# Merge-gate projections of a two-layer encoder in pairs, by seven half-size products

## The chip, the cores and the metric

The kernel runs on one core of a Trainium2 chip. The core has engines that work side by side, each through its own list of instructions in a fixed order: TensorE (PE) multiplies matrices, VectorE (DVE) and ScalarE (ACT) work element by element, GpSimd (POOL) does so too and issues some DMAs, SyncE (SP) issues most DMAs. Operands lie in SBUF, products are summed up in PSUM, the weights and the larger intermediates lie in DRAM. An instruction waits, with all behind it on its engine, until semaphores say that its inputs are there and its buffer is free. The metric is the time of one execution in microseconds (us).

## What is computed

The reference has two layers. In each, all branches read the same normalised input h through one projection, and three sigmoid gates join the branches:

```
h = rmsnorm(x, g_norm)
z = einsum('bsd,dn->bsn', h, w_in)
dq, dk, dv, dg, lq, lk, lv, lg, mq, mg, mgate = split(z, splits)
o_a = diff_attention(...) ; y_a = (rmsnorm(o_a) * (1 - lam_init) * silu(dg)) @ w_br_diff
o_b = dilated groups, combined ; y_b = (o_b * silu(lg)) @ w_br_dil
o_m = memory_attention(...) ; y_m = (o_m * silu(mg)) @ w_br_mem
gates = sigmoid(mgate).reshape(B, S, 3, 1024)
merged = gates[:, :, 0] * y_a + gates[:, :, 1] * y_b + gates[:, :, 2] * y_m
x = x + merged @ w_out
```

There are 512 tokens, a width of 1024 and fp32 throughout; the result is rmsnorm(x, g_final) behind the second layer.

## The kernel before

Each fp32 matrix is kept as two parts, hi and lo, and each product is formed by three matmuls (hi x hi, lo x hi, hi x lo: `mm3`, lines 166 to 169). `split` (lines 94 to 96) makes hi on ACT and lo on DVE. hT, the transposed h, stays in SBUF as hT_hi and hT_lo: 8 blocks of 128 rows with 512 tokens. A projection of 128 columns of w_in (`proj_fm`) is 8 x 3 = 24 matmuls of a 128x128 stationary tile with 512 columns into one PSUM tile. The PSUM tiles with the tag "mm" are 4, taken in turn.

Weights come in the order of `weight_order`. `prefetch` keeps LEAD = 2 weights ahead of the one in use: a DMA into w_raw (3 buffers), w_hi by ACT (4 buffers), w_lo by DVE (3 buffers). A split so waits until PE has done with the weight three or four before it.

A layer has these stages: hT from x; the memory's keys and values; differential, dilated and memory attention woven together, whose results (o_sb, f_osb) go to DRAM in u_d and v_d; and `merge` (lines 580 to 622). `merge` begins with 16 gate projections in U_ORDER, called the U projections below (the U stage). For each, a stored branch result is loaded (u_raw, for 8 of them also a norm u_v with a square root on ACT), the gate is sigmoid on ACT (line 183) and a product on DVE that reads the PSUM tile again (line 184), then u_raw times gate (line 592), u_hi and u_lo. Sigmoid and square root are in different tables of ACT, with a table load at each change. Then come 8 blocks d: three merge-gate projections with a sigmoid each (lines 600 to 604), ya (24 matmuls with w_br_diff), ym and yb (24 matmuls), three products and two sums on DVE, and a split of the sum into mg_hi and mg_lo. `out_proj` multiplies these with w_out.

The Python code yields the instructions; the framework's scheduler, with a model of the times that is used while the kernel is built, decides where each of them stands on its engine, and so also how far the first instructions of the U stage move up among the last ones of attention. In the order, names carry a number for each tile. On the way out of the dilated attention, d_o is its last PSUM tile, and o_sb_5320 (before) or o_sb_5357 (after) the copy of it.

## Time and profile before

| | |
|---|---|
| time, median of 3 runs | 1769.75 us (1768.26 to 1772.07) |
| the profiled execution | 1770.44 us, its span 1768.4 us |
| PE busy | 1743.8 us (99%) |
| DVE, ACT, POOL busy | 1005.5 (57%), 834.5 (47%), 22.1 us (1%) |

Busy time is the time in which an engine executes. PE's matmuls are pipelined, so the durations of neighbours overlap, and what one costs is the distance from its start to the next. An idle engine costs nothing as long as the chain of work that ends last doesn't run over it.

### The profile page before, as it was taken

The page shows a single profiled execution, that of the slowest core. Times are in us where ns is not written, and L with a number is a line of the kernel's source. Part 1 is how long each engine was busy: PE and PEld are TensorE (multiplying, and loading weights), DVE is VectorE, ACT ScalarE, POOL GpSimd, SP SyncE. Part 2 cuts the span into 40 slices and gives each one's busy share as a digit, 9 for nine tenths or more (in the row PEclk, how much of TensorE's full clock was granted, in tenths as well). Part 3 has the DMA queues.
Part 4 walks back from the last instruction along what each step waited for, and adds up shares of the span by engine and source line. Part 5 has one row for each costly group of instructions (what it writes and reads, how often), then busy time and mean ns, then how long its engine had stood idle before and what let it go on. Part 6 is the DMA issues. An engine that isn't in the chain of part 4 may idle for free.

```text
span 1768.4 us, 23429 instructions
## 1 busy us (share of the span) xinstructions
PE 1743.8 (99%) x9012; PEld 1496.0 (85%) x9012; DVE 1005.5 (57%) x1727; ACT 834.5 (47%) x1436; POOL 22.1 (1%) x45
## 2 busy tenths in 40 slices
PE   7999999999999999999999999999999999999998
PEld 6798889888888888888888898888988888888886
DVE  6566576666765663333465656658566747333333
ACT  6455555545555642222255555455454548322223
POOL 2200000000000000000000000000000000000000
PEclk9999999999999999999999999999999999999999
DMA  9643243332432643333572333324332336333342
GB/s 263 141 130 86 72 123 89 103 94 76 117 97 80 202 138 95 97 93 116 160 199 59 112 85 103 94 76 116 95 98 86 101 109 202 107 96 95 96 154 72
DMA packets 308847, 200.26 MB, mean 113 GB/s; under 512 B 14116, under 2 KB 283428, under 8 KB 308736
## 3 DMA queue, kind: packets, MB, share of 16 engines
...
## 4 chain that ended last, share of the span: by engine, by line
PE 97%; DMA 1%; ACT 1%; DVE 0%; issue 0%; SPq 0%; DVEq 0%; ACTq 0%
PE mm L167 27%; PE mm L169 27%; PE mm L168 27%; PE wT_ps L384 2%; PE f_s L407 2%; PE f_s L408 2%; DMA w_raw<-in_w_mem_kv 1%; PE f_o L168 1%; PE f_o L169 1%; PE f_o L167 1%; PE d_o L533 1%; PE d_s L509 1%; PE w_ps L522 0%; PE d_o L168 0%; PE d_o L169 0%; PE d_o L167 0%
## 5 line engine op out<-in xcount | busy, mean ns | idle before, releaser
L96 DVE TENSOR_TENSOR w_lo<-w_raw,w_hi 128x1024 fp32r<-128x1024 f32 (+2 forms) x296 | 335.8, 1135 | 436.1 <-PE mm L169 389.7
L95 ACT ACTIVATE w_hi<-w_raw 128x1024 fp32r<-128x1024 f32 (+2 forms) x296 | 293.3, 991 | 601.5 <-PE mm L168 296.0
L167 PE MATMUL mm<-hT_hi,w_hi 128*128 128x512 f32 x1344 | 529.9, 395 | 1.9 <-ACT hT_hi L95 1.9
L169 PE MATMUL mm<-hT_hi,w_lo 128*128 128x512 f32 x1344 | 527.3, 392 | 0.0
L168 PE MATMUL mm<-hT_lo,w_hi 128*128 128x512 f32 x1344 | 526.7, 392 | 0.0
L167 PEld LDWEIGHTS mm<-hT_hi,w_hi 128*128 128x128 f32 x1344 | 252.8, 188 | 53.2 <-ACT hT_hi L95 2.1
L169 PEld LDWEIGHTS mm<-hT_hi,w_lo 128*128 128x128 f32 x1344 | 252.9, 188 | 53.0 <-DVE w_lo L96 0.4
L168 PEld LDWEIGHTS mm<-hT_lo,w_hi 128*128 128x128 f32 x1344 | 253.0, 188 | 50.7
L169 PE MATMUL mm<-w_hi,hT_lo 128*128 128x384 f32 (+1 forms) x512 | 160.8, 315 | 0.0
L167 PE MATMUL mm<-w_hi,hT_hi 128*128 128x384 f32 (+1 forms) x512 | 160.0, 313 | 0.0
L168 PE MATMUL mm<-w_lo,hT_hi 128*128 128x384 f32 (+1 forms) x512 | 158.5, 310 | 0.0
L413 ACT ACTIVATE f_e<-f_e,f_st 128x512 f32<-128x512 f32 x128 | 91.9, 721 | 49.7 <-DVE f_st L410 49.7
L167 PE MATMUL mm<-u_hi,w_hi 128*128 128x512 f32 x256 | 101.2, 395 | 0.0
L169 PE MATMUL mm<-u_hi,w_lo 128*128 128x512 f32 x256 | 101.2, 395 | 0.0
L168 PE MATMUL mm<-u_lo,w_hi 128*128 128x512 f32 x256 | 101.1, 395 | 0.0
L167 PEld LDWEIGHTS mm<-w_hi,hT_hi 128*128 128x128 f32 x512 | 96.9, 189 | 1.0
L168 PEld LDWEIGHTS mm<-w_lo,hT_hi 128*128 128x128 f32 x512 | 96.8, 189 | 1.1
L169 PEld LDWEIGHTS mm<-w_hi,hT_lo 128*128 128x128 f32 x512 | 96.7, 189 | 0.0
L410 DVE CUSTOM_DVE_ANT_0 f_e<-f_s,f_bias 128x512 f32<-128x512 f32 x128 | 84.4, 681 | 6.8 <-PE f_s L408 6.7
L96 DVE TENSOR_TENSOR f_wTlo<-wT_ps,f_wThi 128x512 fp32r<-128x512 f32 x64 | 43.7, 683 | 31.4 <-ACT f_wThi L95 30.2
L615 DVE TENSOR_TENSOR mgate<-mm,mgate 128x512 f32<-128x512 f32 x48 | 33.0, 688 | 48.4 <-PE mm L169 48.4
L447 DVE RECIPROCAL f_sq<-f_sq 128x512 f32<-128x512 f32 x16 | 53.6, 3349 | 9.5 <-ACT f_sq L446 9.5
(203 smaller groups left out, 2403.9 us busy)
## 6 DMA issues: line engine op xcount, KB each, us to landing
w_raw<-in_w_in SPq DMA_DIRECT2D x168, 512.0 KB, 3.8
...
```

The lines of the kernel that those rows point to most:

```text
L95: nc.scalar.activation(hi, src, AF.Copy)
L96: nc.vector.tensor_tensor(out=lo, in0=src, in1=f32(hi), op=ALU.subtract)
L167: nc.tensor.matmul(o, lhsT=lh, rhs=rh, start=start, stop=False)
L168: nc.tensor.matmul(o, lhsT=lh, rhs=rl, start=False, stop=False)
L169: nc.tensor.matmul(o, lhsT=ll, rhs=rh, start=False, stop=stop)
L384: nc.tensor.transpose(t[:, i], s, ident)
L407: nc.tensor.matmul(sp, lhsT=qh[:, cs], rhs=K[s, m], start=True, stop=False)
L408: nc.tensor.matmul(sp, lhsT=ql[:, cs], rhs=K[s, m], start=False, stop=True)
L410: nc.vector.tensor_tensor_reduce(out=em.rearrange("p (c b) -> p c b", c=4), in0=sp, in1=bt[:, 3 - c:7 - c], op0=ALU.add, op1=ALU.min, scal ...
L413: nc.scalar.activation(em, em, AF.Exp, scale=-1.0, bias=stt[:, m:m + 1], accum_out=stt[:, 2 + m:3 + m])
L447: nc.vector.reciprocal(sq, sq)
L615: nc.vector.tensor_tensor(out=g, in0=y, in1=g, op=ALU.mult)
```

## The change

A pair of merge-gate projections is a product of a matrix of 256 weight columns (2 x 128) and 1024 rows with hT. Cut in halves each way (columns A and B; rows 0 to 511 and 512 to 1023; tokens 0 to 255 and 256 to 511), it is a 2x2 by 2x2 product of blocks, and the change forms it with seven products of blocks in place of eight. Each product has 4 blocks of 128 rows, so 4 x 3 = 12 matmuls with 256 columns.

- `load_pair` loads the four weight blocks of a pair and forms four sums of them on POOL; `prefetch` splits the seven blocks in four parts (three tiles of 1024 elements a partition, one of 512).
- `right_sums` forms the four sums T0 to T3 of blocks of hT on DVE (20 operations) and stores them in t_d in DRAM; it is woven into the attention, but the scheduler puts the operations of it straight behind hT. `right_operands` loads them in 8 tiles t_in in `merge` and splits them (T0hi to T3hi and T0lo to T3lo, each in two halves).
- `pair` adds the products into two tiles on DVE; the sigmoid is taken from there. `merge_steps` orders three pairs and two y steps (ya, ym and yb as before) for two blocks d, and the weights follow that order.
- u_raw, u_v, m and xr share 8 buffers (u_raw and u_v had 3 each). The sums m stay as fp32 until the last pair, and are then split into hT_hi and hT_lo, which `out_proj` reads.

```
+def merge_steps(d0):
+    d1 = d0 + 1
+    return (("pair", (d0, 0), (d0, 1)), ("pair", (d0, 2), (d1, 2)), ("y", d0), ("pair", (d1, 0), (d1, 1)), ("y", d1))
+LAST_PAIR = ((7, 0), (7, 1))
...
+    t_d = dr.tile([4, 2, 128, 2, 256], F32, name="t_d")
...
+    def load_pair(key):
+        l, cols = key[1], key[2:]
+        pool = pair_pool[0]
+        t1, t2, t3 = [pool.tile([128, 8, 128], F32, tag="raw", name="s_raw", bufs=4) if i < 2 else
+                      wp.tile([128, 8, 128], F32, tag="raw", name="s_raw3", bufs=3) for i in range(3)]
+        t4 = pool.tile([128, 4, 128], F32, tag="raw4", name="s_raw4", bufs=2)
+        lo, up = slice(0, 4), slice(4, 8)
+        for t, part, f, k in ((t2, lo, 1, 0), (t3, up, 1, 1), (t1, lo, 0, 0), (t3, lo, 0, 1)):
+            src = w_in[l, k * 512:(k + 1) * 512, cols[f]:cols[f] + 128]
+            dma(t[:, part], src.rearrange("(k p) n -> p k n", p=128))
+        a11, a21, a12, a22 = t1[:, lo], t2[:, lo], t3[:, lo], t3[:, up]
+        tt = nc.gpsimd.tensor_tensor
+        tt(out=t2[:, up], in0=a21, in1=a22, op=ALU.add)
+        tt(out=t1[:, up], in0=t2[:, up], in1=a11, op=ALU.subtract)
+        tt(out=a21, in0=a11, in1=a21, op=ALU.subtract)
+        tt(out=t4, in0=a12, in1=t1[:, up], op=ALU.subtract)
+        for i, t in enumerate((t1, t2, t3, t4)):
+            loaded.append((key + (i,), t))
...
+        if pair_pool and len(loaded) < 3 and order and order[0][0] == "pair":
+            load()
...
+    def pair(l, colA, colB, B, gA, gB):
+        (b11, b21, b22), T = B
+        units = {}
+        def prod(u, part, rhs):
+            if u not in units:
+                units[u] = weight("pair", l, colA, colB, u)
+            (hi, lo), (rh, rl) = units[u], rhs
+            o = mm([128, S], name="s_mm")[:, 0:256]
+            for k in range(4):
+                kk = 4 * part + k
+                mm3(o, hi[:, kk], lo[:, kk], rh[:, k], rl[:, k], k == 0, k == 3)
+            return o
+        add = lambda out, x, y: nc.vector.tensor_tensor(out=out, in0=x, in1=y, op=ALU.add)
+        c11, c12, c21, c22 = gA[:, H0], gA[:, H1], gB[:, H0], gB[:, H1]
+        nc.scalar.activation(c11, prod(0, 0, b11), AF.Copy)
+        add(c12, prod(0, 1, T[1]), c11)
+        add(c21, prod(1, 0, T[2]), c12)
+        o = prod(1, 1, T[0])
+        add(c22, o, c21)
+        add(c12, o, c12)
+        add(c11, prod(2, 0, b21), c11)
+        add(c21, prod(2, 1, T[3]), c21)
+        add(c12, prod(3, 0, b22), c12)
+    H0, H1 = slice(0, 256), slice(256, 512)
+    def right_sums(pool):
+        def acc(out, x, y, op):
+            nc.vector.tensor_tensor(out=out, in0=x, in1=y, op=op)
+        for k2 in range(2):
+            def quarter(kh, ts):
+                ks = slice(4 * kh + 2 * k2, 4 * kh + 2 * k2 + 2)
+                return f32(hT_hi[:, ks, ts]), f32(hT_lo[:, ks, ts])
+            b11, b12, b21, b22 = quarter(0, H0), quarter(0, H1), quarter(1, H0), quarter(1, H1)
+            t1, t2, t3, t4 = [pool.tile([128, 2, 256], F32, tag="ts", name="t_sum", bufs=4) for _ in range(4)]
+            for t, x, y in ((t1, b12, b11), (t3, b22, b12)):
+                acc(t, x[0], y[0], ALU.subtract)
+                yield
+                acc(t, t, x[1], ALU.add)
+                yield
+                acc(t, t, y[1], ALU.subtract)
+                yield
+            for t, x, y in ((t2, b22, t1), (t4, b21, t2)):
+                acc(t, x[0], y, ALU.subtract)
+                yield
+                acc(t, t, x[1], ALU.add)
+                yield
+            for i, t in enumerate((t1, t2, t3, t4)):
+                dma(t_d[i, k2], t)
+            yield
+    def right_operands(pool):
+        T = [[pool.tile([128, 4, 256], F32R, name=f"T{i}{p}") for p in ("hi", "lo")] for i in range(4)]
+        quarter = lambda ks, ts: (hT_hi[:, ks, ts], hT_lo[:, ks, ts])
+        k1, k2 = slice(0, 4), slice(4, 8)
+        yield (quarter(k1, H0), quarter(k2, H0), quarter(k2, H1)), T
+        loads = []
+        for k2 in range(2):
+            for i in range(4):
+                t = pool.tile([128, 2, 256], F32, tag="uT", name="t_in", bufs=32)
+                dma(t, t_d[i, k2])
+                loads.append((T[i], slice(2 * k2, 2 * k2 + 2), t))
+        yield
+        for (hi, lo), ks, t in loads:
+            split(hi[:, ks], lo[:, ks], t)
+            yield
...
     def merge(l, yu, ym, lam_init):
         U = {}
-        for i in U_ORDER:
-            raw = yu.tile([128, S], F32, tag="ul", name="u_raw", bufs=3)
+        pair_pool[:] = [yu]
+        rop = right_operands(yu)
+        B = next(rop)
+        m_tile = lambda name: ym.tile([128, S], F32, tag="m", name=name, bufs=8)
+        for n, i in enumerate(U_ORDER):
+            next(rop, None)
+            raw = m_tile("u_raw")
             dma(raw, u_d[i])
             if i < 8:
-                v = yu.tile([128, S], F32, tag="uv", name="u_v", bufs=3)
+                v = m_tile("u_v")
                 dma(v, v_d[i])
...
+        M, G = [], {}
+        for d0 in range(0, 8, 2):
+            for step in merge_steps(d0):
+                if step[0] == "pair":
+                    gA, gB = [sg_tile(name="mgate") for _ in range(2)]
+                    pair(l, *[MGATE + b * 1024 + d * 128 for d, b in step[1:]], B, gA, gB)
+                    for g in (gA, gB):
+                        nc.scalar.activation(g, g, AF.Sigmoid)
+                    G[step[1]], G[step[2]] = gA, gB
+                    if step[1:] == LAST_PAIR:
+                        for e, m in enumerate(M):
+                            split(hT_hi[:, e], hT_lo[:, e], m)
+                    continue
+                d = step[1]
+                gs = [G.pop((d, b)) for b in range(3)]
...
+                m = m_tile("m")
+                nc.vector.tensor_tensor(out=m, in0=gs[0], in1=gs[2], op=ALU.add)
+                M.append(m)
+                if d == 7:
+                    split(hT_hi[:, d], hT_lo[:, d], m)
+        pair_pool[:] = []
...
-                            mm3(os[c], M[kk][0][:, cs], M[kk][1][:, cs], whi[:, k], wlo[:, k], kk == 0, kk == 7)
+                            mm3(os[c], hT_hi[:, kk, cs], hT_lo[:, kk, cs], whi[:, k], wlo[:, k], kk == 0, kk == 7)
...
-                xr = ym.tile([128, 512], F32, tag="xr", name="xr", bufs=2)
+                xr = ym.tile([128, 512], F32, tag="m", name="xr", bufs=8)
...
-                fp, _ = weave((diff_proj(l, j + 1, P), 8), (dil_att(l, j, P, dp), 4))
+                gens = [(diff_proj(l, j + 1, P), 8), (dil_att(l, j, P, dp), 4)]
+                if j == 1:
+                    gens.append((right_sums(al), 22))
+                fp = weave(*gens)[0]
...
-    nc = bacc.Bacc("TRN2", target_bir_lowering=False, num_devices=1)
+    nc = bacc.Bacc("TRN2", target_bir_lowering=False, num_devices=1, dynamic_dma_scratch_size=2048)
```

In this order all rows are of layer 0; layer 1 has them alike. The first place is ACT where the attention ends and the U stage begins. Before, from o_sb, the copy of the last dilated attention result, on:

```order
L189 ACTIVATE o_sb_5320<-d_o_5181 128x512
L95 ACTIVATE u_hi_5394<-u_raw_5357 128x512
L183 ACTIVATE gate_5648<-mm_5623 128x512
L95 ACTIVATE u_hi_5435<-u_raw_5398 128x512
L183 ACTIVATE gate_5693<-mm_5668 128x512
L95 ACTIVATE w_hi_5795<-w_raw_5793 128x1024
```

After, from the instruction behind o_sb on:

```order
L105 ACTIVATE w_hi_5872<-w_raw_5870 128x1024
L105 ACTIVATE T0hi_5394<-t_in_5402 128x512
L105 ACTIVATE T1hi_5396<-t_in_5404 128x512
L105 ACTIVATE T2hi_5398<-t_in_5406 128x512
L105 ACTIVATE T3hi_5400<-t_in_5408 128x512
L105 ACTIVATE T0hi_5394<-t_in_5410 128x512
L105 ACTIVATE T1hi_5396<-t_in_5412 128x512
L105 ACTIVATE w_hi_5913<-w_raw_5911 128x1024
L105 ACTIVATE T2hi_5398<-t_in_5414 128x512
L105 ACTIVATE T3hi_5400<-t_in_5416 128x512
L105 ACTIVATE u_hi_5455<-u_raw_5418 128x512
L303 ACTIVATE gate_5721<-mm_5696 128x512
```

The first u_hi and the sigmoid of the 7th U projection (gate_5648 before, gate_5721 after) moved behind two weight splits and eight T splits.

The second place is DVE at the same point. Before, from the weight split of the 11th U projection on:

```order
L96 TENSOR_TENSOR w_lo_5710<-w_raw_5707,w_hi_5709 128x1024
L592 TENSOR_TENSOR u_raw_5357<-u_raw_5357,gate_5390 128x512
L592 TENSOR_TENSOR u_raw_5398<-u_raw_5398,gate_5431 128x512
L96 TENSOR_TENSOR u_lo_5395<-u_raw_5357,u_hi_5394 128x512
L184 TENSOR_TENSOR gate_5648<-mm_5623,gate_5648 128x512
L592 TENSOR_TENSOR u_raw_5439<-u_raw_5439,gate_5472 128x512
```

After, from the last but two of the first six T splits on, with the weight split of the 13th U projection, w_lo_5873:

```order
L106 TENSOR_TENSOR T3lo_5401<-t_in_5408,T3hi_5400 128x512
L106 TENSOR_TENSOR T0lo_5395<-t_in_5410,T0hi_5394 128x512
L106 TENSOR_TENSOR T1lo_5397<-t_in_5412,T1hi_5396 128x512
L106 TENSOR_TENSOR w_lo_5873<-w_raw_5870,w_hi_5872 128x1024
L106 TENSOR_TENSOR T2lo_5399<-t_in_5414,T2hi_5398 128x512
L717 TENSOR_TENSOR u_raw_5418<-u_raw_5418,gate_5451 128x512
L106 TENSOR_TENSOR T3lo_5401<-t_in_5416,T3hi_5400 128x512
L717 TENSOR_TENSOR u_raw_5461<-u_raw_5461,gate_5494 128x512
L717 TENSOR_TENSOR u_raw_5504<-u_raw_5504,gate_5537 128x512
L717 TENSOR_TENSOR u_raw_5547<-u_raw_5547,gate_5580 128x512
L106 TENSOR_TENSOR u_lo_5456<-u_raw_5418,u_hi_5455 128x512
L304 TENSOR_TENSOR gate_5721<-mm_5696,gate_5721 128x512
```

The gate product of the 7th U projection, behind which PE's 11th may write the PSUM tile, stood four places behind the weight split of the 11th and now stands eight places behind that of the 13th.

## Rows read from the trace of the kernel before

**Rows 1.** The page: busy time of engines, and the chain of waits.
```profile
PE 1743.8 (99%) x9012; PEld 1496.0 (85%) x9012; DVE 1005.5 (57%) x1727; ACT 834.5 (47%) x1436; POOL 22.1 (1%) x45
...
PE 97%; DMA 1%; ACT 1%; DVE 0%; issue 0%; SPq 0%; DVEq 0%; ACTq 0%
```

**Rows 2.** PE timeline, U stage: start us, duration us, engine, line, operation, out<-in, count.
```profile
584.51 0.40 PE L169 MATMUL mm<-hT_hi,w_lo 128*128 128x512 f32 x1
...
589.99 0.39 PE L169 MATMUL mm<-hT_hi,w_lo 128*128 128x512 f32 x1
```

**Rows 3.** PE timeline, attention of layer 0: matmuls of 256 columns.
```profile
303.66 0.28 PE L168 MATMUL f_o<-f_wTlo,f_vhi 128*128 128x256 f32 x1
303.78 0.28 PE L169 MATMUL f_o<-f_wThi,f_vlo 128*128 128x256 f32 x1
...
304.85 0.28 PE L169 MATMUL f_o<-f_wThi,f_vlo 128*128 128x256 f32 x1
```

**Rows 4.** DVE by line and form: count, busy us, mean ns, idle before and releaser.
```profile
L96 DVE TENSOR_TENSOR w_lo<-w_raw,w_hi 128x1024 fp32r<-128x1024 f32 x232 | 283.0, 1221 | 324.6 <-PE mm L169 289.3 <-PE mm L168 22.0 <-issue 9.2
...
L96 DVE TENSOR_TENSOR u_lo<-u_raw,u_hi 128x512 fp32r<-128x512 f32 x32 | 22.0, 687 | 9.3 <-ACT u_hi L95 9.0
...
L96 DVE TENSOR_TENSOR f_vlo<-mm,f_vhi 128x256 fp32r<-128x256 f32 x32 | 13.3, 420 | 3.2 <-ACT f_vhi L95 2.8
```

**Rows 5.** ACT by line and form, same columns.
```profile
L95 ACT ACTIVATE w_hi<-w_raw 128x1024 fp32r<-128x1024 f32 x232 | 245.9, 1060 | 447.0 <-issue 175.4 <-PE mm L168 163.4 <-PE mm L169 78.6
...
L603 ACT ACTIVATE mgate<-mm 128x512 f32<-128x512 f32 x48 | 27.8, 578 | 0.0
...
L588 ACT ACT_TABLE_LOAD x10 | 12.8, 1283 | 0.2
...
L95 ACT ACTIVATE f_vhi<-mm 128x256 fp32r<-128x256 f32 x32 | 11.9, 384 | 3.4 <-PE mm L169 2.7
```

**Rows 6.** ACT timeline, U stage of layer 0; idle before and releaser in brackets.
```profile
584.25 0.60 ACT L189 ACTIVATE o_sb<-d_o 128x512 f32<-128x512 f32 x1 [0.26 <-PE d_o L533]
585.02 0.63 ACT L95 ACTIVATE u_hi<-u_raw 128x512 fp32r<-128x512 f32 x1 [0.18 <-DVE u_raw L592]
585.56 0.58 ACT L183 ACTIVATE gate<-mm 128x512 f32<-128x512 f32 x1
...
588.88 1.06 ACT L95 ACTIVATE w_hi<-w_raw 128x1024 fp32r<-128x1024 f32 x1 [1.73 <-issue]
...
610.72 0.63 ACT L588 ACTIVATE u_v<-u_v 128x512 f32<-128x512 f32 x1 [3.10 <-DMA u_v<-v_d]
```

**Rows 7.** DVE timeline, U stage of layer 0.
```profile
583.16 1.23 DVE L96 TENSOR_TENSOR w_lo<-w_raw,w_hi 128x1024 fp32r<-128x1024 f32 x1 [6.43 <-PE mm L169]
584.30 1.29 DVE L592 TENSOR_TENSOR u_raw<-u_raw,gate 128x512 f32<-128x512 f32 x2
...
586.30 0.68 DVE L184 TENSOR_TENSOR gate<-mm,gate 128x512 f32<-128x512 f32 x1
...
631.13 0.69 DVE L589 SCALAR_TENSOR_TENSOR u_raw<-u_raw,u_v 128x512 f32<-128x512 f32 x1 [1.21 <-DMA u_raw<-u_d]
...
637.33 0.68 DVE L184 TENSOR_TENSOR gate<-mm,gate 128x512 f32<-128x512 f32 x1
```

**Rows 8.** SP timeline: DMA issues at the start of the U stage.
```profile
577.22 1.05 SPq L584 DMA_DIRECT2D u_raw<-u_d  x2
```

**Rows 9.** Busy us of PE, PEld, DVE, ACT, POOL in a window, clock, DMA share, GB/s.
```profile
590.00:596.00 6.00, 6.00 (x28) 4.99 (x27) 3.42 (x6) 5.93 (x7) 0.00 (x0) 1.00 1.09 343
```

**Rows 10.** POOL timeline: its selection at the start.
```profile
3.20 0.31 POOL masks.py:199 TENSOR_SCALAR_AFFINE_SELECT ident<-ident 128x128 f32<-128x128 f32 x1
```

**Rows 11.** Windows near the start of layer 0, columns as in rows 9.
```profile
44.00:48.50 4.50, 2.61 (x17) 1.97 (x15) 4.10 (x7) 3.03 (x6) 0.00 (x0) 1.00 0.72 203
48.50:51.90 3.40, 3.40 (x10) 2.62 (x9) 0.42 (x1) 0.00 (x0) 2.36 (x4) 0.50 0.80 146
51.90:56.00 4.10, 4.10 (x19) 3.39 (x18) 0.00 (x0) 0.00 (x0) 0.00 (x0) 1.00 0.72 139
```

More of the change, by code (lines that the diff above doesn't have):

```diff
@@ L145, in encoder_kernel @@
     order = list(weight_order())
-    ready = []
-    def prefetch(n):
-        while len(ready) < n and order:
-            key, k, cols, pieces = order.pop(0)
-            raw = wp.tile([128, k, cols], F32, tag="raw", name="w_raw", bufs=3)
-            for k0, k1, c0, c1, src in pieces:
-                dma(raw[:, k0:k1, c0:c1], src.rearrange("(k p) n -> p k n", p=128))
-            hi = wp.tile([128, k, cols], F32R, tag="hi", name="w_hi", bufs=4)
-            lo = wp.tile([128, k, cols], F32R, tag="lo", name="w_lo", bufs=3)
+    loaded, ready = [], []
@@ new lines, in encoder_kernel, with load @@
+    pair_pool = []
+    def load():
+        if order[0][0] == "pair":
+            load_pair(order.pop(0))
+            return
+        key, k, cols, pieces = order.pop(0)
+        raw = wp.tile([128, k, cols], F32, tag="raw", name="w_raw", bufs=3)
+        for k0, k1, c0, c1, src in pieces:
+            dma(raw[:, k0:k1, c0:c1], src.rearrange("(k p) n -> p k n", p=128))
+        loaded.append((key, raw))
+    def load_pair(key):
[16 more added lines that the diff above has]
+            loaded.append((key + (i,), t))
@@ L156, in prefetch @@
+    def prefetch(n):
+        while len(ready) < n and (loaded or order):
+            if not loaded:
+                load()
+            key, raw = loaded.pop(0)
+            shape = list(raw.shape)
+            hi = wp.tile(shape, F32R, tag="hi", name="w_hi", bufs=4)
+            lo = wp.tile(shape, F32R, tag="lo", name="w_lo", bufs=3)
             split(hi, lo, raw)
             ready.append((key, hi, lo))
+        if pair_pool and len(loaded) < 3 and order and order[0][0] == "pair":
+            load()
@@ L622, in merge @@
-        return M
-    def out_proj(l, M, done):
+        M, G = [], {}
+        for d0 in range(0, 8, 2):
+            for step in merge_steps(d0):
+                if step[0] == "pair":
+                    gA, gB = [sg_tile(name="mgate") for _ in range(2)]
[6 more added lines that the diff above has]
+                            split(hT_hi[:, e], hT_lo[:, e], m)
+                    continue
+                d = step[1]
+                gs = [G.pop((d, b)) for b in range(3)]
+                whi, wlo = weight("ba", l, d)
+                ya = mm([128, S])
+                for k in range(8):
+                    mm3(ya, whi[:, k], wlo[:, k], U[k][0], U[k][1], k == 0, k == 7)
+                whi, wlo = weight("bm", l, d)
+                ym_ps = mm([128, S])
+                yb = mm([128, S])
+                for k in range(8):
+                    mm3(ym_ps if k < 4 else yb, whi[:, k], wlo[:, k], U[8 + k][0], U[8 + k][1], k % 4 == 0, k % 4 == 3)
+                for g, y in zip(gs, (ya, yb, ym_ps)):
+                    nc.vector.tensor_tensor(out=g, in0=y, in1=g, op=ALU.mult)
+                nc.vector.tensor_tensor(out=gs[0], in0=gs[0], in1=gs[1], op=ALU.add)
+                m = m_tile("m")
[3 more added lines that the diff above has]
+                    split(hT_hi[:, d], hT_lo[:, d], m)
@@ L625, in out_proj @@
+        pair_pool[:] = []
+    def out_proj(l, done):
         for n in range(2):
@@ L678, in encoder_kernel @@
     lams = []
-    M = ym_c = ym = None
+    ym_c = ym = None
     for l in range(DEPTH):
@@ L705, in done @@
                 dma(x1_d[c][:, ns], xt[c][:, ns])
-            out_proj(l - 1, M, done)
+            out_proj(l - 1, done)
             close(ym_c)
@@ L739, in encoder_kernel @@
         ym_c, ym = opened(f"ym{l}", "right")
-        M = merge(l, yu, ym, lam_init)
+        merge(l, yu, ym, lam_init)
         close(yu_c)
@@ L769, in done @@
         dma(out_v[c][:, h1], y[:, h1])
-    out_proj(DEPTH - 1, M, done)
+    out_proj(DEPTH - 1, done)
     close(ym_c)
```

39 lines of the change are left out of this document (6 added, 33 removed).

## The prediction

> **What bounds the kernel now.** The page's first part and the chain of waits come first [rows 1]: TensorE (PE) is busy 99% of the 1768.4 us span and 97% of the chain that ended last is PE; VectorE (DVE) has 57%, ScalarE (ACT) 47%. So a saving on PE shows in full unless something makes PE wait. Second, the timeline of PE, for what one matmul costs: the pitch from start to start, since the listed durations of neighbours overlap [rows 2, 3]. Third, the timelines of ACT, DVE and SP around the start of the gate stage (583 to 640 us), because an average hides that stage: there ACT is almost full.
>
> The profiled execution took 1770.44 us, of which 1768.4 is the span; the median of the runs shown is 1769.75, 0.7 lower. I sum against 1770.4 and take 0.7 off at the end.
>
> **What PE saves.** One 128x512 projection is 24 matmuls; from 584.51 to 589.99 lie 24 starts, 5.48 us, 0.228 each [rows 2]. Two gate projections are 48 matmuls, 10.96 us. The change makes them 7 products x 4 k x 3 = 84 matmuls of 128x256. From 303.66 to 304.85 ten such starts lie 0.119 apart, each with another stationary tile, as in the products [rows 3]: 84 x 0.119 = 10.00 us. A pair saves 0.96 us; 12 pairs in each of 2 layers: -23.0 us. The pitch for 256 columns is more than half of that for 512, so 7/8 of the columns brings 8.8%, not 12.5%.
>
> **What is added on other engines in the steady part of the merge.** Operations that follow at once start about 0.08 us (DVE: 583.16 to 584.30 for 1.22) to 0.09 us (ACT: 585.02 to 585.56 for 0.63) sooner than the listed duration, and I count so [rows 4 to 7]. Per pair: DVE 3.5 weight splits (3 x 1.14 + 0.61) and 7 PSUM additions of 256 columns at 0.42 = 7.0 us; ACT 3.4 us of w_hi, one copy of 0.4 and two sigmoids of 0.58 = 5.0 us; both under the 10.0 us of PE. A y step adds 5.3 us of DVE beside 10.96 us of PE. PE stays the bound there: cost 0, covered by 3.0 us of slack per pair on DVE; were the cover gone, each us over 10 would cost 24 us in all. After the last pair of a layer seven splits of m stand in a row: 7 x 0.61 = 4.3 us against about 3.5 us free: 0.8 us a layer.
>
> POOL gets 4 additions of 128x512 a pair, and the trace has none like them. From below the DVE's 0.69 us for that shape [rows 4], from above four times the 0.31 us of POOL's one select of 128x128, 1.25 us [rows 10]. I take 1.25, as the row on that engine: 5.0 us of each 10, and the loads are a pair ahead: cost 0. From 2.5 us each POOL would be the bound.
>
> The Trainium skill (GPSIMD Engine Reference, 3.1) gives an addition of two fp32 inputs with 2048 elements 4497 ns there, 1.96 times DVE; with its own ratio 512 columns are an estimate of 1.3 us, so the sum would not change by it; no run here shows it yet.
>
> hT's sums are 20 DVE operations of 512 columns a layer, 20 x 0.61 = 12.2 us, and 8 stores. In layer 0 the order puts them directly behind hT, where DVE's windows are empty (0.00 busy of 4.1 us) [rows 11]; what doesn't fit there delays the first q/k eviction, 0 to 2 us; I take 1 in all. Their stores stand in SP's queue between weight loads that are issued well ahead: 0. The smaller ring for POOL's DMAs concerns 45 POOL instructions at the start, whose DMAs are not waited for by PE: 0.
>
> **What is moved: the block of T splits ahead of the U stage.** This is the term that decides. ACT and DVE execute in a fixed order. Before, behind o_sb at 584.25 came u_hi at 585.02 and the gate sigmoids at once [rows 6], on DVE the gate product of the 7th U projection at 586.30 [rows 7]. Now ACT runs w_hi_5872, six T splits, w_hi_5913, two T splits and only then u_hi_5455 and gate_5721 (the 7th projection); DVE runs six T splits, w_lo_5873, T2lo, u_raw_5418, T3lo, three u_raw, u_lo_5456, gate_5721. The splits need t_in, 8 loads of 256 KB that wait until PE is through with d_o (about 584: o_sb, which reads it, starts at 584.25) and stand in SP's queue ahead of the u_raw loads, two of which were issued at 577.22 before [rows 6, 8].
>
> First wait. w_hi_5872 waits for the buffer of the 9th projection, whose end is 588.88 (ACT's w_hi there is released by it) [rows 6]; w_hi_5913 and w_lo_5873 wait for those of the 10th, which ends 5.48 later, at D = 594.3. The 8 loads are 2.1 MB; at the 343 GB/s seen in 590 to 596 that is 6 us behind 585, about 592, so six splits are done by D [rows 9]. Then: w_hi_5913 from D+0.25 to D+1.25, T2hi to D+1.8, T2lo to D+2.5, then seven DVE operations of 0.61 (u_raw, T3lo, 3 u_raw, u_lo, gate_5721): D+6.8. PE's 11th projection needs the PSUM tile of the 7th (4 tiles), which gate_5721 frees: PE, which never waits here now, stands 6.8 us in each layer. If the u_raw loads land later than D+3 it is more: 1.75 MB behind t_in at the same rate is 597, D+3, so up to 3 us more.
>
> Second wait. Behind it lies the rest of the chain on ACT and DVE: 15 u_hi, 10 gates, 8 u_v, 6 w_hi, 10 table loads of 1.28: 15 x 0.54 + 10 x 0.49 + 8 x 0.54 + 6 x 0.96 + 12.8 = 35.9 us of ACT, hand in hand with DVE. Before, the same chain ran from 585.02 to 638.01 (last gate product, 637.33 + 0.68), 53.0 us, with PE through with its 16th projection at 588.88 + 7 x 5.48 = 627.2: ACT and DVE trailed by 11 us, and four PSUM tiles of 5.48 us hid it. Now the chain starts at D+3.1 = 597.4, 12.4 later, and the 4th product of the first pair, 3 x 1.43 us behind the 16th projection, wants the tile of the 16th gate at 631.5, since a tile of the pairs lasts 1.43 us. At the old pace the chain would end at 650.4, 19 us late. Its transfers were waited for (3.1 us at 610.72, 1.2 at 631.13) [rows 6, 7]; eight tiles instead of three let them start sooner, 4 us gained: 646.4, and 15 us late. With no idle time on ACT (35.9 us: 633.3) only the first wait of 6.8 is left, since PE itself is then late by it. So 6.8 to 19 a layer; I take 15, near the row of this very chain. The first wait is part of this, not added. After PE stood 1.9 of the 4.5 us from 44.0, its granted clock was 0.50 (1.2 GHz) for 3.4 us [rows 11], 1.7 us of work lost; here the chain is late anyhow and hides it. Layer 1 has the same order: 2 x 15 = 30 us.
>
> **Sum.** 1770.4 - 23.0 + 30 + 2 x 0.8 + 1 = 1780.0; less 0.7: 1779.3, so 1779.
>
> **Rivals.**
> A, only the first wait: the chain runs without idle time. 1770.4 - 23.0 + 2 x 6.8 + 2.6 = 1763.6, up to 1770 with late u_raw loads. For it: transfers start sooner and ACT's sum is 36 us. Against: gate products wait for sigmoids, these for table loads, and ACT and DVE hand over at each U.
> B, the gain in full: the splits cost nothing. 1770.4 - 23.0 + 2.6 = 1750. For it: DVE is at 57%. Against: the order itself; w_lo_5873 cannot run before the 10th projection ends, and eight operations lie between it and the tile that PE wants.
> C, slower by POOL's sums: at 3 us each (2.4 times the row of POOL) a pair takes 12 us in place of 10 and PE waits 2 us in each: 24 x 2 = 48 on top of A, 1812; it decides from 2.5 us. The rows bear it out little: POOL's only data operations take 0.2 to 0.3 us.
> D, the exclusion between POOL and DVE: DVE's splits, which read two tiles of SBUF, and POOL's sums shut each other out. Splits of 4.0 us and sums of 5.0 a pair make 9.0 of 10 us, so it decides only where waits come at bad moments: DVE at 7.0 + 5.0 = 12 us at worst, 2 us a pair, 48 us, again about 1812; half of it 1788 from A, 1803 from the forecast. No stretch of this trace has POOL and DVE busy with data together for long, so rows say nothing against it. The Trainium skill (SBUF — State Buffer, "Who interferes with whom") states such an exclusive lock for a DVE instruction with two SBUF inputs against a POOL instruction that reads SBUF.
> E, the change doesn't save: 84 weight loads of 0.19 us would bind at 15.8 us a pair. Rows 3 have a new weight tile at each 0.119 us, so very little.
>
> **How the numbers follow.** Forecast 0.53 (1774 to 1789), A 0.22, B 0.10, C and D 0.12, E 0.03. A measurement can tell 0.2%, 3.5 us: faster is below 1766.2, slower above 1773.3. Faster: B and half of A, 0.21. Same: half of A and the forecast's lower edge, 0.16. Slower: 0.63. The range leaves out B and the far part of C, D and E: 1760 to 1797, low end under A's 1763, high end over the forecast's 19 us a layer with a share of D.
>
> **What would show it.** Right: PE pitch 0.119 in the pairs; a hole of PE of 6.8 to 10 us ahead of the 11th U projection near 594, released by DVE's gate product; holes in the first pair, released by the gate products of the 15th and 16th; none in the later pairs; the same in layer 1. Wrong: no hole near 594 (B); a hole there and none in the first pair (A); POOL additions of over 2 us, or PE waiting in every pair for w_lo or Pool (C, D).

## The result and the profile after

The changed kernel takes 1782.2 us (median; 1780.83 to 1784.06) against 1769.95 (1768.26 to 1772.07) before: ratio 1.0069, 95% interval 1.0052 to 1.0087, slower by 12 us. The forecast was 1779 with a range of 1760 to 1797. The profiled execution spans 1779.9 us, before 1768.4; the tables below account for this difference of 11.5.

Four marks on PE (the starts of the last d_o matmul and of the first y matmul of each layer) and the end of the span give it stage by stage. "Lost" is what the distances from one matmul's start to the next exceed the regular pitch by, added up.

| stretch | before, us | after, us | difference | lost after |
|---|---|---|---|---|
| start to the last d_o matmul of layer 0 | 583.93 | 589.16 | +5.23 | 5.2 more than before |
| to the first y matmul of layer 0 (U stage, first pairs) | 59.63 | 78.70 | +19.07 | 15.8 |
| to the last d_o matmul of layer 1 | 809.11 | 793.07 | -16.04 | 0 in the pairs |
| to the first y matmul of layer 1 | 59.32 | 78.61 | +19.29 | 15.6 |
| to the end of the span | 256.37 | 240.34 | -16.03 | 0 in the pairs |

The second and fourth stretch hold more gate work after than before (two pairs in place of three projections), so only their "lost" says what went wrong there. PE's starts price the rest. Before, a block's three merge-gate projections (first start, and the start behind them) and then `out_proj` of layer 0, likewise:

```profile
654.77 0.40 PE L167 MATMUL mm<-hT_hi,w_hi 128*128 128x512 f32 x1
...
671.13 0.40 PE L167 MATMUL mm<-u_hi,w_hi 128*128 128x512 f32 x1
...
847.69 0.40 PE L167 MATMUL mm<-w_hi,mg_hi 128*128 128x512 f32 x1
...
892.48 0.28 PE L167 MATMUL mm<-mT_hi,w_hi 128*128 128x256 f32 x1
```

After, the second pair of layer 0 and `out_proj`:

```profile
657.89 0.28 PE L213 MATMUL s_mm<-hT_hi,w_hi 128*128 128x256 f32 x1
...
667.86 0.40 PE L213 MATMUL mm<-u_hi,w_hi 128*128 128x512 f32 x1
...
857.20 0.39 PE L213 MATMUL mm<-w_hi,hT_hi 128*128 128x512 f32 x1
...
900.74 0.28 PE L213 MATMUL mm<-mT_hi,w_hi 128*128 128x256 f32 x1
```

Three projections took 16.36 us, so two took 10.91; a pair takes 9.97. 24 pairs save 22.4 us. The 192 matmuls of `out_proj`, which now read hT_hi and hT_lo in place of mg_hi and mg_lo, take 43.54 us in place of 44.79, which saves 2.5 us in the two layers; why they are faster was not tried. Against these 24.9 us, 5.2 + 15.8 + 15.6 = 36.6 us are lost: +11.7, with 11.5 measured.

The page after: busy us (share of the span) and instructions of each engine, then the shares of the chain of waits.

```profile
PE 1730.8 (97%) x9876; PEld 1526.6 (86%) x9876; DVE 1182.7 (66%) x1999; ACT 893.9 (50%) x1524; POOL 192.9 (11%) x141
...
PE 89%; DVE 4%; DMA 3%; ACT 2%; issue 2%; SPq 0%; ACTq 0%; DVEq 0%
```

Beside [rows 1], PE's share falls from 99% to 97% and its part of the chain from 97% to 89%: PE now waits. PE's own waits (who waits for whom: us in total, times, longest) say for what; these are the larger ones that the kernel before doesn't have.

```profile
PE mm L213 <- DVE gate L304: 12.9, 2, 6.5
...
PE mm L215 <- DVE w_lo L106: 6.2, 2, 3.4
PE mm L213 <- DVE b_t L350: 2.8, 1, 2.8
...
PE s_mm L213 <- ACT mgate L242: 1.5, 2, 1.0
PE b_ps L348 <- DVE m_ql L578: 1.1, 1, 1.1
```

Two kinds come twice, once a layer: the gate product and a weight split. The timeline of PE shows the first of them in layer 0 (start, duration, engine, line, operation, idle time before and its releaser).

```profile
599.29 0.39 PE L215 MATMUL mm<-hT_hi,w_lo 128*128 128x512 f32 x1
606.16 0.80 PE L213 MATMUL mm<-hT_hi,w_hi 128*128 128x512 f32 x1 [6.48 <-DVE gate L304]
```

6.87 us from start to start, 6.6 above the pitch of [rows 2]. This is the 11th U projection, which wants the PSUM tile of the 7th. The DVE timeline shows what stands ahead of that tile's gate product:

```profile
600.08 1.22 DVE L106 TENSOR_TENSOR w_lo<-w_raw,w_hi 128x1024 fp32r<-128x1024 f32 x1
601.21 0.68 DVE L106 TENSOR_TENSOR T2lo<-t_in,T2hi 128x512 fp32r<-128x512 f32 x1
601.81 0.69 DVE L717 TENSOR_TENSOR u_raw<-u_raw,gate 128x512 f32<-128x512 f32 x1
602.41 0.69 DVE L106 TENSOR_TENSOR T3lo<-t_in,T3hi 128x512 fp32r<-128x512 f32 x1
603.02 1.89 DVE L717 TENSOR_TENSOR u_raw<-u_raw,gate 128x512 f32<-128x512 f32 x3
604.82 0.68 DVE L106 TENSOR_TENSOR u_lo<-u_raw,u_hi 128x512 fp32r<-128x512 f32 x1
605.43 0.68 DVE L304 TENSOR_TENSOR gate<-mm,gate 128x512 f32<-128x512 f32 x1
```

w_lo needs the weight buffer of the 10th projection (its last matmul starts at 599.29) and follows a T split that ends at 600.16. Behind it the row runs without a gap to the gate product, whose end at 606.11 releases PE. The windows of both holes (stretches in which PE stands idle), of what follows each, and of a steady stretch (window, its length, busy us of PE, PEld, DVE, ACT, POOL, granted clock, DMA share, GB/s):

```profile
599.50:606.10 6.60, 0.18 (x1) 0.00 (x0) 6.60 (x11) 5.56 (x10) 0.00 (x0) 0.87 1.08 366
606.10:610.90 4.80, 4.74 (x11) 3.77 (x12) 4.17 (x8) 4.74 (x6) 0.00 (x0) 0.50 1.22 290
610.90:616.00 5.10, 5.10 (x23) 4.13 (x23) 3.83 (x7) 3.73 (x6) 0.00 (x0) 0.98 1.04 350
636.30:639.20 2.90, 0.16 (x1) 0.00 (x0) 2.90 (x3) 2.87 (x5) 2.90 (x3) 0.87 0.00 0
639.20:645.30 6.10, 6.04 (x14) 4.80 (x15) 6.10 (x9) 3.48 (x5) 1.15 (x1) 0.50 0.31 86
684.00:699.00 15.00, 15.00 (x87) 13.08 (x86) 9.56 (x11) 5.29 (x6) 14.01 (x8) 1.00 0.38 110
```

After each hole the granted clock is 0.50 (1.2 GHz) for 4.8 and 6.1 us, with a pitch of 0.43 in place of 0.228. So the first wait costs 6.6 + 2.4 = 9.0 us in layer 0; the second 3.0 + 2.9, and 0.7 more in the first pair, 6.6. The last row is the steady merge: PE full at full clock, DVE busy for 9.56 of 15 us, POOL for 14.01.

In the second hole POOL is busy throughout, and DVE's operations there are long:

```profile
633.50 1.79 DVE L717 TENSOR_TENSOR u_raw<-u_raw,gate 128x512 f32<-128x512 f32 x1
635.21 1.78 DVE L106 TENSOR_TENSOR u_lo<-u_raw,u_hi 128x512 fp32r<-128x512 f32 x1
636.92 2.28 DVE L106 TENSOR_TENSOR w_lo<-w_raw,w_hi 128x1024 fp32r<-128x1024 f32 x1
639.12 1.77 DVE L106 TENSOR_TENSOR u_lo<-u_raw,u_hi 128x512 fp32r<-128x512 f32 x1
640.82 0.68 DVE L304 TENSOR_TENSOR gate<-mm,gate 128x512 f32<-128x512 f32 x1
```

POOL's sums at the same time (two of four), and one of them alone:

```profile
634.82 1.63 POOL L186 TENSOR_TENSOR s_raw<-s_raw 128x512 f32<-128x512 f32 x1
636.41 1.71 POOL L187 TENSOR_TENSOR s_raw<-s_raw 128x512 f32<-128x512 f32 x1
...
715.41 1.29 POOL L185 TENSOR_TENSOR s_raw<-s_raw,s_raw 128x512 f32<-128x512 f32 x1 [16.82 <-DVE mgate L240]
```

Operations of DVE that read two tiles of SBUF take 1.78 and 2.28 us where the same lines take 0.68 and 1.22 thirty microseconds earlier, with POOL idle. The second hole ends with the w_lo that took 2.28. A product that reads PSUM and SBUF isn't lengthened. The gate product at 640.82 comes after the last sum (638.08 to 640.34) and doesn't show it, but the steady merge does, with a sum of POOL and a product of DVE in it:

```profile
695.05 2.28 POOL L187 TENSOR_TENSOR s_raw<-s_raw 128x512 f32<-128x512 f32 x1
```

```profile
696.09 0.68 DVE L747 TENSOR_TENSOR mgate<-mm,mgate 128x512 f32<-128x512 f32 x1
```

The loss in the start stage is one wait of DVE (its timeline, layer 0):

```profile
53.53 0.69 DVE L257 TENSOR_TENSOR t_sum<-hT_hi,t_sum 128x512 f32<-128x512 f32 x1
60.19 0.69 DVE L257 TENSOR_TENSOR t_sum<-hT_hi 128x512 f32<-128x512 f32 x1 [5.97 <-DMA t_d<-t_sum]
```

The second half of hT's sums needs the t_sum buffers of the first half. SP issued the first of their stores at 51.59, and DVE goes on at 60.19, when it has landed, 8.6 us later. PE then stands twice, from 66.62 to 71.08, for the DVE work behind it (b_t and m_ql in the list of waits).

### The profile page after: what moved, and what is told of

The parts are those of the page before. It is cut to its first block, busy times and chain, and to the rows that moved or that the text cites. A ratio compares the mean times of both kernels' runs of the same rounds, so it can differ in the third digit from the quotient of the medians.

```text
span 1779.9 us, 26114 instructions
## 1 busy us (share of the span) xinstructions
PE 1730.8 (97%) x9876; PEld 1526.6 (86%) x9876; DVE 1182.7 (66%) x1999; ACT 893.9 (50%) x1524; POOL 192.9 (11%) x141
## 4 chain that ended last, share of the span: by engine, by line
PE 89%; DVE 4%; DMA 3%; ACT 2%; issue 2%; SPq 0%; ACTq 0%; DVEq 0%
PE mm L213 20%; PE mm L215 20%; PE mm L214 20%; PE s_mm L213 4%; PE s_mm L215 4%; PE s_mm L214 4%; PE wT_ps L504 2%; PE f_s L527 2%; PE f_s L528 2%; DVE u_raw L717 1%; PE f_o L214 1%; PE f_o L213 1%; PE f_o L215 1%; PE d_o L653 1%; PE d_s L629 1%
## 5 line engine op out<-in xcount | busy, mean ns | idle before, releaser
L213 PE MATMUL mm<-hT_hi,w_hi 128*128 128x512 f32 x960 | 384.6, 401 | 17.5 <-DVE gate L304 12.9
L215 PE MATMUL mm<-hT_hi,w_lo 128*128 128x512 f32 x960 | 382.0, 398 | 6.2 <-DVE w_lo L106 6.2
L214 PE MATMUL mm<-hT_lo,w_hi 128*128 128x512 f32 x960 | 381.5, 397 | 0.0
L213 PEld LDWEIGHTS mm<-hT_hi,w_hi 128*128 128x128 f32 x960 | 183.3, 191 | 56.7 <-DVE gate L304 13.8
L215 PEld LDWEIGHTS mm<-hT_hi,w_lo 128*128 128x128 f32 x960 | 183.3, 191 | 44.9 <-DVE w_lo L106 7.0
L215 PE MATMUL mm<-w_hi,hT_lo 128*128 128x384 f32 (+2 forms) x640 | 210.1, 330 | 0.0
L213 PE MATMUL mm<-w_hi,hT_hi 128*128 128x384 f32 (+2 forms) x640 | 209.7, 328 | 0.0
L214 PE MATMUL mm<-w_lo,hT_hi 128*128 128x384 f32 (+2 forms) x640 | 208.3, 326 | 0.0
L105 ACT ACTIVATE w_hi<-s_raw 128x1024 fp32r<-128x1024 f32 x96 | 91.2, 950 | 168.6 <-PE mm L214 97.7
L106 DVE TENSOR_TENSOR w_lo<-s_raw,w_hi 128x1024 fp32r<-128x1024 f32 x96 | 116.1, 1209 | 34.4 <-issue 34.4
```

The costliest lines, as they stand in the source:

```text
L105: nc.scalar.activation(hi, src, AF.Copy)
L106: nc.vector.tensor_tensor(out=lo, in0=src, in1=f32(hi), op=ALU.subtract)
L213: nc.tensor.matmul(o, lhsT=lh, rhs=rh, start=start, stop=False)
L214: nc.tensor.matmul(o, lhsT=lh, rhs=rl, start=False, stop=False)
L215: nc.tensor.matmul(o, lhsT=ll, rhs=rh, start=False, stop=stop)
```

## The experiments

"Before" is the kernel before on the same chip, "lost" is per layer (layer 0 / layer 1) between the last d_o and the first y matmul, as in the table: 15.8 / 15.6 in the changed kernel. Two theories stood after the result. One: both waits of a layer come from the order, because the moved splits start the gate chain 12 us late (first u_hi 13.4 us behind the last d_o, before 1.1). Two: the order makes the first wait, and POOL's sums, which hold DVE up, make the second.

**e1_ts7: seven buffers for t_sum.**

```
-  t1, t2, t3, t4 = [pool.tile([128, 2, 256], F32, tag="ts", name="t_sum", bufs=4) for _ in range(4)]
+  t1, t2, t3, t4 = [pool.tile([128, 2, 256], F32, tag="ts", name="t_sum", bufs=7) for _ in range(4)]
```

> Only edit: the sums of hT get 7 buffers (t_sum) in place of 4. The changed kernel reaches the end of layer 0's attention 5.2 us later than before, and its DVE waits 5.97 us at 60.19 us for the stores of the first four sums. Theory one (the second half of the sums waits for buffers whose stores stand behind weight loads in SP's queue, and DVE, in order, holds up the bias tables that PE needs at 68 us): the wait and PE's holes of 1.4 and 3.1 us go, 1782.2 - 5 = 1777 us, and d_o's end in layer 0 is back within 1 us of 583.9. Rival (the 12.2 us of additional DVE work delay the tables, with or without buffers): the holes stay at over 3 us, 1780 to 1782.

1778.2 us against 1771.78, ratio 1.0036 [1.0023, 1.005]. The last d_o matmul of layer 0 starts at 582.43 (589.16 in the changed kernel), and DVE's sums follow at once:

```profile
54.02 0.69 DVE L257 TENSOR_TENSOR t_sum<-hT_hi,t_sum 128x512 f32<-128x512 f32 x1
54.63 1.29 DVE L257 TENSOR_TENSOR t_sum<-hT_hi 128x512 f32<-128x512 f32 x2
```

The buffers were the cause of the loss at the start. That the stores stood behind weight loads, as the expectation says, is wrong: in the changed kernel SP issued the first three from 51.59 to 53.88, as their sums were done, and they took 7.6 to 8.6 us to land, while POOL's queue held 43.9% of the DMA engines' time and SP's 19.6% (50 to 62 us). Which of the two queues slowed the stores was not tried. The merge still lost 15.6 / 17.5.

**e2_no_pool: no sums on POOL; seven loads a pair in place of four.**

```
-        for t, part, f, k in ((t2, lo, 1, 0), (t3, up, 1, 1), (t1, lo, 0, 0), (t3, lo, 0, 1)):
+        for t, part, f, k in ((t2, lo, 1, 0), (t3, up, 1, 1), (t1, lo, 0, 0), (t3, lo, 0, 1),
+                              (t2, up, 1, 1), (t1, up, 0, 1), (t4, lo, 0, 1)):
-        tt(out=t2[:, up], in0=a21, in1=a22, op=ALU.add)
...
```

> Left out: the four weight sums on POOL; seven blocks are loaded as they are (the pair's products are of unsummed weights), so POOL does no data operation in the merge. DVE's operations beside the sums took 1.7 us in place of 0.69 at 620 to 640 us. Theory one (contention of POOL and DVE stretches the U stage's tail and makes the second hole of PE, 3.2 us of waiting and its half-clock stretch): DVE's operations are back at 0.69, the second hole near 636 (layer 0) and 1507 (layer 1) goes, 6 us a layer, about 1770; the first hole of 6.8 us near 600 stays. Rival (ACT and DVE are late by the T splits alone, as the prediction had it): the second hole stays, within 2 us of 1782.

1778.34 against 1771.78, ratio 1.0035 [1.0022, 1.0048]; lost 12.4 / 14.8; the time lies between the two expectations. The second hole in the U stage was gone, but 3.4 / 6.4 us were now lost in the first pair. The three more loads a pair changed the queue as well, so this run doesn't price POOL; e10_memset does.

**e3_no_t: T neither loaded nor split; the products read quarters of hT.**

```
-        yield (quarter(k1, H0), quarter(k2, H0), quarter(k2, H1)), T
-        loads = []
...
+        b11, b21, b22 = quarter(k1, H0), quarter(k2, H0), quarter(k2, H1)
+        yield (b11, b21, b22), (b11, b21, b22, b11)
```

> Left out: the loads and the splits of T in the merge (blocks of hT stand in for T in the products); hT's sums and their stores stay, and the weight sums on POOL stay. Theory one (the block of eight splits ahead of the U stage makes the first hole and, by the late start of the chain behind it, the second): both holes go, 16 us a layer, 1750 us. Rival (the second hole is made by POOL's sums): the first hole goes with its half-clock stretch, 9 us a layer, DVE's operations stay at 1.7 us beside POOL's, a hole of 2 us or more stays ahead of the first pair, 1760 to 1766.

1774.53 against 1771.78, ratio 1.0016 [1.0007, 1.0026]; lost 10.0 / 10.6: above both theories' numbers. Without any T work the first u_hi still came 9.3 / 10.1 us behind d_o, because u_raw, not T, was late. SP's timeline (start, time to issue, line, DMA):

```profile
591.94 1.89 SPq L182 DMA_DIRECT2D s_raw<-in_w_in  x3
593.87 2.46 SPq L699 DMA_DIRECT2D u_raw<-u_d  x5
```

Before, two u_raw loads left at 577.22 [rows 8]; here they stand behind s_raw loads of the first pair. So the order costs something on SP's queue too, beside the splits.

**e4_paced: T loaded into the ring of u_raw, one split behind each of the last eight U.**

```
-                t = pool.tile([128, 2, 256], F32, tag="uT", name="t_in", bufs=32)
+                t = mp.tile([128, 2, 256], F32, tag="m", name="t_in", bufs=8)
...
+            if n >= 8:
+                next(rop, None)
```

> Only the place of T's loads and splits is changed: each t_in shares the 8 buffers of u_raw and is loaded and split behind one of the last eight U projections, so the splits stand between those of the U stage on ACT and DVE, none ahead of the 7th gate. Theory one (place, not amount): the first hole of PE near 600 and 1471 us goes, 9 us a layer; what the second becomes depends on POOL: between 1752 (goes too) and 1766 (stays). Rival (the amount of added work on ACT and DVE in this stage is what PE waits for, wherever it stands): the lost time moves to the first pair, over 1776.

1784.99 against 1771.78, ratio 1.0074 [1.0059, 1.0089]; lost 16.5 / 15.5. The first hole was gone, and as much time was lost later: 11 to 12 us a layer in the first pair and most of the rest at the 16th projection (the w_lo row):

```profile
PE s_mm L213 <- ACT mgate L242: 6.0, 4, 2.6
PE mm L215 <- DVE w_lo L106: 5.5, 2, 3.0
PE s_mm L214 <- DVE T1lo L106: 4.6, 2, 2.6
```

Here the place of the splits only chose where PE waits. The rival's time (over 1776) came true; whether its reason, the amount of work, did, needed e11_paced_memset.

**e5_singles: four gates of a layer single, 10 pairs a layer; the pairs start three projections later.**

```
+    if d0 < 0:
+        return (("one", (0, 0)), ("one", (0, 1)), ("one", (0, 2)), ("y", 0))
+    if d0 == 7:
+        return (("one", (7, 2)), ("pair", (7, 0), (7, 1)), ("y", 7))
...
-        for d0 in range(0, 8, 2):
+        for d0 in (-1, 1, 3, 5, 7):
```

> Only the merge order is changed: the three gate projections of block 0 (behind the U stage) and one of block 7 are single ones of 24 matmuls with 512 columns, as before; 10 pairs a layer stay of 12, which gives back 4 x 1.0 us of PE's saving. T's block of splits, hT's sums and POOL's sums stay as in the changed kernel. Theory one (ACT and DVE trail PE by some 11 us at the end of the U stage also before, hidden there by PSUM tiles that last 5.5 us; a pair right behind it, with 1.4 us a tile, lays it bare): with 16 us of single projections behind the U stage the waits there and in the first pair go, the first hole of 6.8 us with its half-clock stretch stays: 1782 + 4 - 13 = 1773. Rival (PE must wait for the amount of work on ACT and DVE, whatever follows): 1782 to 1786.

1774.0 against 1770.18, ratio 1.0017 [1.0008, 1.0027], with 1773 expected. The first hole stays (6.6 us, and 2.7 at half clock), the second is gone; lost 9.4 / 9.2. Three tiles of 5.5 us ahead of the first pair give the chain the time it lacks, and POOL's sums no longer fall into it.

**e6_no_t_pool: e2_no_pool and e3_no_t together.**

```
(the edits of e2_no_pool and e3_no_t)
```

> Left out: T's loads and splits in the merge (blocks of hT stand in) and POOL's weight sums (unsummed blocks are loaded). Without T alone 10 us a layer were still lost between the end of attention and the first ya. Theory one (lag laid bare: 11 us at the 16th gate less 4.3 us until the 4th product): 6 to 7 us a layer stay, all in the first pair, and 1764 to 1766 is the time (1782.2 less 2 x 9). Rival (the rest without T is POOL's contention): under 2 us a layer stay, 1754. Second rival (POOL's sums play no part): 10 us a layer stay, within 2 us of the run without T.

1771.1 against 1770.18, ratio 1.0005 [0.9996, 1.0015]; lost 8.8 / 8.7. The time lies between the expectations (1766 and 1774). Not conclusive: its seven s_raw loads a pair stand ahead of u_raw in SP's queue, the first u_hi came 12.1 us behind d_o, and the first hole came back.

**e7_best: singles, T split behind the U stage, seven t_sum.**

```
+        return (("one", (0, 0)), ("one", (0, 1)), ("one", (0, 2)), ("y", 0))
...
-                t = pool.tile([128, 2, 256], F32, tag="uT", name="t_in", bufs=32)
+                t = mp.tile([128, 2, 256], F32, tag="m", name="t_in", bufs=8)
...
+                    for _ in range(4):
+                        next(rop, None)
```

> A version for both causes and the start: single projections of block 0 behind the U stage (10 pairs a layer), T loaded into the buffers of u_raw and split behind the U stage's last gates, 7 buffers for hT's sums. Theory one (lag laid bare, T's block, the wait for the sums' stores): no hole of over 1 us in the merge, no wait at 60 to 70 us; 1770 - 20 x 1.0 + 2 = 1752, at most 1758. Rival (amount): lost time of over 8 us a layer ahead of the first pair, over 1765.

**1749.0 us** (1746.52 to 1749.62) against 1770.18: ratio 0.9874 [0.9857, 0.989]. It beats both kernels. Its windows, columns as above:

```profile
590.00:630.00 40.00, 40.00 (x178) 33.13 (x177) 33.41 (x50) 37.41 (x48) 0.00 (x0) 1.00 0.89 271
630.00:644.00 14.00, 14.00 (x64) 11.59 (x63) 13.73 (x20) 10.26 (x17) 3.34 (x1) 1.00 0.61 187
```

PE is full through the U stage and the first single gates, at full clock, with POOL idle in the U stage. From the last d_o to the first y matmul it takes 59.32 us in each layer, as the kernel before (59.63 and 59.32): nothing is lost. The gain of 21.2 us is that of the 20 pairs, 18.7, and the 2.5 of `out_proj`.

**e8_own_u: e3_no_t, with u_raw and u_v in rings of their own, so that their loads start early.**

```
-            raw = m_tile("u_raw")
+            raw = yu.tile([128, S], F32, tag="ul", name="u_raw", bufs=3)
```

> Left out: T's loads and splits, as in the run without T (blocks of hT stand in). Changed beside that: u_raw and u_v have 3 buffers each of their own again, in the pool of the gate stage, and SP issues three u_raw loads ahead of the pairs' weights. In the run without T the first u_raw times gate stood 8.5 to 9.4 us behind the last d_o matmul (0.4 before the change), and 10 us a layer were lost. Theory one (u_raw loaded late, behind s_raw, delays the chain, and the late chain meets short PSUM tiles): the first product comes at 6.5 us or sooner, the hole of 1.7 to 2.6 us at the 11th projection goes, the 16th gate product comes at 53 us in place of 56, and 5 to 7 us a layer are lost: 1764 to 1768. Rival (only POOL's sums and the amount of work count): 10 us a layer again, 1774.

1773.38 against 1770.1, ratio 1.0018 [1.0009, 1.0028]. The first u_hi came 7.0 us behind d_o and the first hole was gone, yet 9.7 / 9.7 us were lost, all in the first pair, and DVE's operations beside POOL still took 1.78: the rival's number (1774) came true, and theory one's 5 to 7 us a layer did not.

**e9_11pairs: e7_best with one pair more a layer.**

```
-        return (("one", (0, 0)), ("one", (0, 1)), ("one", (0, 2)), ("y", 0))
+        return (("one", (0, 0)), ("one", (0, 1)), ("pair", (0, 2), (7, 2)), ("y", 0))
```

> The version with single projections behind the U stage, with two of them in place of three (blocks 0, 0 and 0, 1) and none for block 7: 11 pairs a layer. Theory one (some 5 to 6 us of lag at the 16th gate need 11 us of single projections at most): no hole, 1749 - 2 x 1.0 = 1747. Rival (the third single was needed): holes of 2 us or more in the first pair, 1749 or over.

1753.01 (1749.96 to 1753.92) against 1770.1, ratio 0.9898 [0.9884, 0.9913]: it lost 2.9 / 3.8 us, most of it in the first pair, more than the 0.93 a layer that the pair saves. The rival's time (1749 or over) was right, though no single hole reached its 2 us. Three singles are the better number here.

**e10_memset: POOL writes the four blocks with a constant in place of the sums; the order on all other engines is the same row for row.**

```
-        tt(out=t2[:, up], in0=a21, in1=a22, op=ALU.add)
-        tt(out=t1[:, up], in0=t2[:, up], in1=a11, op=ALU.subtract)
-        tt(out=a21, in0=a11, in1=a21, op=ALU.subtract)
-        tt(out=t4, in0=a12, in1=t1[:, up], op=ALU.subtract)
+        ms(t2[:, up], 0.5)
+        ms(t1[:, up], 0.5)
+        ms(a21, 0.5)
+        ms(t4, 0.5)
```

> Left out: the arithmetic of POOL's four weight sums; in their place POOL fills the same four blocks with a constant, so that it writes and doesn't read. The loads, the waits and the order of ACT, DVE and SP are those of the changed kernel, row for row. Theory one (POOL's reads and DVE's operations with two inputs from SBUF exclude each other, which lengthens these from 0.68 to 1.77 us): all DVE operations are at 0.69 and 1.22 us, the 16th gate product comes at 59 us behind d_o in place of 63.4, some 4 us a layer are won: 1782.2 - 8 = 1774. Rival (POOL's writes count as much, or the run without sums was faster for another reason, its loads): DVE's operations stay at 1.7 us beside POOL's, 1780 or over.

1770.55 against 1769.37, ratio 1.0004 [0.9995, 1.0014]; lost 9.8 / 9.5; theory one expected 1774. The first hole is as it was (6.6 us, and 2.7 at half clock), the second is gone with its w_lo wait, and the 16th gate product comes 57.3 us behind d_o in place of 63.4. In the changed kernel eight DVE operations ahead of that product are lengthened in each layer, by 8.7 us together; here none is. DVE by line and form (count, busy us, mean ns, idle before): first the changed kernel, then this one.

```profile
L106 DVE TENSOR_TENSOR w_lo<-s_raw,w_hi 128x1024 fp32r<-128x1024 f32 x72 | 99.7, 1385 | 34.4 <-issue 34.4
...
L106 DVE TENSOR_TENSOR u_lo<-u_raw,u_hi 128x512 fp32r<-128x512 f32 x32 | 28.2, 887 | 3.0 <-ACT u_hi L105 2.8
```

```profile
L106 DVE TENSOR_TENSOR w_lo<-s_raw,w_hi 128x1024 fp32r<-128x1024 f32 x72 | 87.6, 1217 | 57.3 <-issue 53.3 <-PE mm L215 4.0
...
L106 DVE TENSOR_TENSOR u_lo<-u_raw,u_hi 128x512 fp32r<-128x512 f32 x32 | 21.7, 684 | 3.0 <-ACT u_hi L105 2.8
```

Against its own "before" the changed kernel is at +12.2 us and this one at +1.2: POOL's sums cost 11 us, some 6 a layer, though in the mean over all its calls a u_lo or w_lo is only 0.2 us longer.

**e11_paced_memset: e4_paced and e10_memset together.**

```
(the edits of e4_paced and e10_memset)
```

> The kernel with T's splits placed behind the last eight U projections, with POOL filling the four blocks with a constant in place of summing (left out: the sums' arithmetic). Rows of ACT, DVE and SP as in the paced kernel. That one lost 16 us a layer, as much as the changed kernel, though its first hole was gone. Theory one (place and POOL's reads each cost: the block's first hole 9 us a layer, the exclusion 6 us): the exclusion goes here too, the 16th gate product comes at 53 us in place of 59, and 4 to 8 us a layer are lost, most of it in the first pair: 1785 - 18 = 1767, 1762 to 1770. Rival (the amount of splits in this stage holds PE wherever they stand): over 12 us a layer, 1776 or over.

1770.14 against 1770.61, ratio 0.9998 [0.9989, 1.0008]; lost 8.2 / 9.0, nearly all in the first pair, for mgate, T1lo and T2hi. That is the upper edge of what the expectation's theory one (theory two above) gave, and the rival's 1776 is out. All engines but POOL have their rows in the order of e4_paced, which was at +13.2 us against its own "before"; this one is at -0.5. So POOL's sums cost 13.7 us there, about half of what e4_paced lost. What is left, 8.2 / 9.0, is little under the 9.8 / 9.5 of e10_memset: moving the splits alone wins little.

## Why the forecast was right, and where its reasons were not

The number came true (1782.2 against 1779, within the range), with the sign. By the steps of the sum:

- **Pairs, -23.0: -22.4.** A pair takes 9.97 us, and the two projections replaced took 10.91. Right; the two times lie 0.03 and 0.05 us below those worked out.
- **`out_proj`, not in the sum: -2.5.** Its new operands made its matmuls faster, which no term held.
- **Start, 1: 5.2.** Mis-sized. I asked whether 20 operations fit into DVE's gap and took their stores at 0 because of the weight loads around them in SP's queue. The four buffers made the sums of the second half wait until the first stores had landed (5.97 us), which no term held. e1_ts7 takes it away.
- **First wait, 6.8: 6.6 and 2.4.** The hole, its place, its releaser and the seven DVE operations ahead of it are as worked out. One reading under it was not in its row: the w_hi of [rows 6] at 588.88 names "issue" as its releaser and not PE. In the changed kernel the w_hi at that place, at 594.10, waits 4.03 us for PE, so the time was right. The step that failed is "here the chain is late anyhow and hides it": the 2.4 us at half clock were lost in full. e10_memset shows them with the second hole gone.
- **Second wait, 15 in all with the first: 15.8 and 15.6.** Right as a sum, by luck, and wrong in its reason. I put it down to the chain's late start, with ACT and DVE at the pace of before less 4 us, and had the last gate product end at 646.4, 62.5 us behind d_o. Without the sums the chain is faster than that: in e10_memset it ends at +58.0, and PE loses only 0.4 and 1.05 us in the first pair, because PE itself is 9 us late by then. With them it ends at +64.1. The 6 us came from POOL's sums, which stretch the two-input operations of DVE in the last U projections; the row that PE waited for was the 16th projection's w_lo and not a gate product of the pairs.
- **POOL's sums, cost 0: 11 us.** Their length was taken well for a sum alone (1.25; 1.29), but the mean of all 96 is 1.80, 7.2 us a pair in place of 5.0. In the steady pairs they cost nothing, as said: PE is full there with POOL busy for 14.01 of 15 us. The failed step is "the loads are a pair ahead: cost 0", which looked at POOL as a bound and not at what it does to DVE. Rival D had the mechanism and priced it in the 24 steady pairs, where 3 us of slack on DVE cover it. It decides in the one stretch where DVE has no slack, the end of the U stage.
- **0.8 a layer at the last pair: 0.** No wait is there.

The Trainium skill (SBUF — State Buffer, "Who interferes with whom") states that a DVE instruction with two SBUF inputs contends with a GpSimd instruction that reads SBUF, and not with one that only writes. The traces agree on each side: 1.78 us in place of 0.68 beside the sums, 0.68 for the product that reads PSUM, 0.68 beside memsets.

What stays open: how much of the 10 us that e3_no_t and e8_own_u lose without any T work is POOL's (they were not run with memsets, and e6_no_t_pool changed the queue), why the first stores of t_sum took over 7 us, and why `out_proj` is faster.
